# Ten input-projection pairs that copy their first and fifth product from bank to bank, nine of them with ten of sixteen k-tiles by sevens

## The chip, the cores and the metric

The kernel runs on one core of one Trainium2 chip. The metric is device microseconds of one execution, the median of several runs; lower is better. The engines are TensorE (PE for matmuls, PEld for its weight loads), VectorE (DVE), ScalarE (ACT), GpSimd (POOL) and SyncE (SP, which issues most of the loads). PSUM has eight banks of 128 x 512 float32; a matmul writes into one bank.

## What is computed

One layer of a decoder trunk on 256 rows of 2048 channels: a norm, one large input projection, three attention mixers side by side, gates, an output projection, then a gated feed-forward. The change lies in the input projection and in what takes its results:

```
h = rmsnorm(x, g_mix)
proj = h @ w_in                      # 256 x 2048 times 2048 x 12288
q, k, v = qkv[0], qkv[1], qkv[2]     # 16 heads of 128 each, in four groups of four
gates = sigmoid(proj[..., 3 * MIX_WIDTH:])   # three branches of 2048
...
merged = gates[0]*(o_a @ w_branch_a) + gates[1]*(o_b @ w_branch_b) + gates[2]*(o_c @ w_branch_c)
x = x + merged @ w_out
```

## The kernel before

**Products.** Rows are two tiles of 128 (t = 0, 1), the 2048 input channels are sixteen k-tiles of 128, output columns go in blocks of 512. Every operand is split into a high and a low part (`split`, L107: the cast to the high part on ScalarE, the difference as the low part on VectorE), and one product (`product`, L169) is three matmuls: high by high, high by low, low by high. A weight block of two k-tiles (128 x 1024) is split in one go by `parts` (L311); its parts lie in the tiles w_hi and w_lo, of which there are five each, and a tile is free again when its last product is done.

**Pairs.** Two blocks of 512 columns, A and B, are projected together by `project_pair` (L351). For eight of the sixteen k-tiles (chunks 0 and 1, `WC`) it uses seven products in place of eight for each two-by-two block of (row tile, k half) by (k half, column block): sums of weights are formed on VectorE, or by DMAs that add (tiles u, g_raw), and sums of the activations lie ready in `hs` (class `Both`, L294). In the code `form(bank, f, ...)` is product number f = 1 to 7, four products at a time (two chunks, two k-tiles); `rest` is a plain product of a weight block, four products (two k-tiles, two row tiles). The order is 1, 2, 5, two rests of column B, 6, a rest, 7, a rest, 3, two rests of column A, 4, two rests. That makes seven times four and eight times four, 60 products in a pair.

**Banks.** A pair has four banks: X and Y, in which column A ends, and Z and V, in which column B is put together. Before `acc2` is opened all four come from the pool `acc`, which has two banks named ps and two named qs: the Z and V of a pair are the two banks that were X and Y of the pair before (`in_turn`, L874). Product 1 is needed in X and in the end in Y, product 5 in Z and V. In the pairs of w_in, X and Z are copied to SBUF by ScalarE (`snapshot`, L326: s1 and z5), and VectorE adds them back later: L407 and L408 for column B, and L423 for c11 = Y + s1, which is the first half of the result. In the pairs of w_gu and w_out (`by_banks`, L348) ScalarE copies from bank to bank instead, Y from X (L376) and V from Z (L378), and the sums are finished in PSUM.

**Units.** The projection runs two blocks of 512 columns alone (v of head group 0, one gate), then eleven pairs: q and k of group 0 (called qk0 here), qk1, v of groups 1 and 2 (vv), qk2, qk3, v of group 3 with a gate (vg), and five pairs of gates (g1 to g5). Before g4 the attention's banks are closed and `acc2` gives Z and V banks of their own. `begin_pair` (L338) does the start of the next pair (loads, the splits of the first block, sums u, splits of the second) at the end of the one before.

**What runs beside.** Attention is cut into steps, which `parts` sets off one by one (`stages`, `slow_stages`). `keep_qk` (L845) takes the q and k results, `rows_to_columns` (L758) scales, normalizes and transposes them, `keep_v` (L828) takes v. The tile v has one buffer: v of group 1 is written (L838) when the last matmul of group 0's attention (L708, L709) has read the old one. `keep_gate_rows` (L810) applies the sigmoid and sends a gate out to memory. `split_o` (L881) splits the attention's output during g4 and g5.

**What sets the order.** The framework orders each engine's instructions at build time, by the program's order and by what would be ready in its own model of the times; some are pinned to the program's order (`keep_in_program_order`), all loads by SP among them (`fetch`, L103). On the chip each engine runs its list strictly in order and waits on semaphores.

Of the kernel before, what the change touches and what calls it, by code (L numbers as in the profile page):

```python
# [55 lines left out]
def hybrid_block(ctx: ExitStack, tc: tile.TileContext, x, w_in, w_branch, w_out, w_gu, w_down, rel_bias,  # L56
# [237 lines left out]
    class Both(Sums):  # L294


        def __init__(self, pl, cols, wc):
            super().__init__(pl, "b", wc, False)
            self.shared(pl)
            self.plain = cols.plain  # L300


    WC = (0, 1)

    def load(w, k, col0, pl=None):

        raw = pl.tile([P, 2, NB], F32, name="g_raw", bufs=6 if pl is gx else 4) if pl else wpool.tile([P, 2, NB], F32, name="w_raw", bufs=4)
        (nc.sync.dma_start if w is w_down else fetch)(raw, block(w, k, col0))
        return raw
# [27 lines left out]

    def begin_pair(acts, w, colA, colB):  # L338

        b11, b12 = (quarter(acts, w, 0, col0) for col0 in (colA, colB))  # L340
        p11 = [parts(b) for b in b11]
        u = [gx.tile([P, 2, NB], F32, name="u") for _ in acts.wc]
        for a, b, d in zip(b11, b12, u):
            nc.vector.tensor_add(d, a, b)  # L344
        b21 = quarter(acts, w, 1, colA)
        return p11, b12, u, b21, [parts(b) for b in (u if by_banks(w) else b21)]

    def by_banks(w):  # L348
        return w is w_gu or w is w_out

    def project_pair(acts, w, colA, colB, begun=None, nxt=None, by_dma=False, early=None):  # L351
# [7 lines left out]
        def form(ps, f, srcs, start, stop, split=False):  # L359
            for i, c in enumerate(acts.wc):  # L360
                wh, wl = srcs[i] if split else parts(srcs[i])
                for j in range(2):
                    product(ps, *acts.form(f, c, j), wh[:, j], wl[:, j], start and i + j == 0,
                            stop and i + j == len(acts.wc))
# [8 lines left out]
        p11, b12, u, b21, second = begun or begin_pair(acts, w, colA, colB)  # L373
        form(X, 1, p11, True, True, True)
        if by_banks(w):
            tc.keep_in_program_order(nc.scalar.copy(Y, X))  # L376
            form(Z, 5, second, True, True, True)
            doubled[:] = [tc.keep_in_program_order(nc.scalar.copy(V, Z))]  # L378
            form(Y, 2, b21, False, False)
        else:  # L380
            s1 = snapshot(X)
            form(Y, 2, second, True, False, True)
            form(Z, 5, u, True, True)
# [6 lines left out]
        rest(1, ks[0], Z, V, start=not by_banks(w), raw=plain[0])  # L390
# [6 lines left out]
        rest(1, ks[2], Z, V)  # L397
        if not by_dma:
            add_into(b12, b22)
        form(X, 7, b12, False, True)  # L400
        x3 = snapshot(X)
        rest(1, ks[3], Z, V, stop=True)
        c22 = half_kb()
        if by_banks(w):
# [4 lines left out]
        form(Z, 3, b22, False, True)  # L409
# [6 lines left out]
        form(X, 4, u, False, False)  # L416
# [3 lines left out]
        if by_banks(w):  # L420
# [59 lines left out]
    for c in range(2, 4):  # L480
        whole[c] = gx.tile([P, NT, 4, P], F32, name="g_raw", bufs=6)
# [104 lines left out]
    def load_rows():  # L586
        for t in range(NT):
            for n in range(2):
                rows.append(gx.tile([P, 2 * NB], F32, name="g_raw", bufs=6))
# [168 lines left out]
    def rows_to_columns(g, sbs, dst):  # L758
        for i in (0, 2, 3):
# [85 lines left out]
    def keep_qk(g, q0, q1, k0, k1):  # L845
        sbs = [q0, half_kb(), k0, k1]
        nc.scalar.activation(sbs[1], q1, AF.Copy, scale=rstd[:, 1:2])
# [16 lines left out]
    def pair_of(kind, what):  # L864
# [6 lines left out]
        if kind == "vg":  # L871
            return hs, w_in, V0 + what[0] * NB, gate_col(*what[1])

# [15 lines left out]
    for (kind, what), after in zip(units, units[1:] + [(None, None)]):  # L889
# [47 lines left out]
    pgx.close()  # L937
    tc.keep_in_program_order(nc.scalar.preload_act_table_set("natural_log_exp_and_others"))
# [372 lines left out]
```

## Time and profile before

| | |
|---|---|
| median of 3 runs | 1338.33 us (1338.18 to 1339.57) |
| the profiled execution | 1337.34 us |
| its span, first to last instruction | 1335.6 us |
| matmul instructions | 6243 |
| loads of w_in by SP | 103 + 88 of 512 KB |
| adding DMAs by POOL, into u, and into g_raw at L389 | 50 and 20 of 512 KB |

The profile is of one execution. Its views: the page (busy time of each engine, forty slices, the chain of work that ended last), groups of instructions by line, the timeline of an engine in a window, and a table of windows: for each stretch of time its length, then the busy time of each engine with the number of instructions in brackets, the granted TensorE clock, the share of the DMA engines and their GB/s. Busy times of neighbouring instructions overlap a little, so a price is read from start to start where instructions follow each other without a gap.

### The profile page before, as it was taken

Reading aid. Unit: us, or ns where it says so; the run is one execution under the profiler, and the core shown is the slowest. Engines: PE = TensorE matmul, PEld = TensorE weight load, DVE = VectorE, ACT = ScalarE, POOL = GpSimd, SP = SyncE. Lnnn points to the kernel's source line nnn. Section 1 sums busy time; section 2 is a strip of 40 time slices with the busy share of each in tenths; the row PEclk is TensorE's granted clock in tenths of the full one; section 3 lists DMA queues with packets and bytes.
Section 4 is the critical chain, followed back from the end, with each engine's and each line's share of the span. In section 5 each row is a group of like instructions: output and inputs, shape, how many; then the busy total and the mean of one; then the engine's idle time right before and its main releaser. Section 6 shows DMA issues by size and latency. Waiting matters only on the chain.

```text
span 1335.6 us, 17783 instructions
## 1 busy us (share of the span) xinstructions
PE 1328.6 (99%) x6243; PEld 1158.7 (87%) x6243; DVE 1168.9 (88%) x1254; ACT 940.9 (70%) x1209; POOL 130.9 (10%) x195
## 2 busy tenths in 40 slices
PE   9999999999999999999999999999999999999998
PEld 6888888888888888888888888888888888888887
DVE  7978898989888897986999999989899997998887
ACT  7786867788777776544777778777877875665563
POOL 1100110001111111100210000001000001001010
PEclk9999999999999999999999999999999999999999
DMA  9997878797788878877988889889899977789883
GB/s 359 308 282 246 263 210 258 252 277 223 263 267 282 277 241 289 294 249 244 305 312 267 259 265 278 238 252 308 279 286 274 281 216 253 252 276 301 270 271 96
DMA packets 119505, 354.70 MB, mean 266 GB/s; under 512 B 32832, under 2 KB 34552, under 8 KB 119416
## 3 DMA queue, kind: packets, MB, share of 16 engines
q1 hardware_dynamic: 77016, 277.45, 58.4%
q0 software_dynamic: 19984, 69.76, 22.2%
q10 hardware_dynamic: 22416, 6.36, 2.8%
q8 instruction: 49, 0.80, 0.2%
q14 instruction: 40, 0.33, 0.1%
HBM read 294.26 MB, written 14.70 MB: 231 GB/s over the span
## 4 chain that ended last, share of the span: by engine, by line
PE 98%; DMA 1%; ACT 0%; DVE 0%; SPq 0%; issue 0%; DVEq 0%
PE qs L172 12%; PE ps L173 12%; PE qs L174 12%; PE qs L173 12%; PE ps L174 12%; PE ps L172 12%; PE z L173 4%; PE z L172 4%; PE z L174 4%; PE v L172 2%; PE v L173 2%; PE v L174 2%; PE tr L174 1%; PE tr L172 1%; PE tr L173 1%; PE tr L205 1%
## 5 line engine op out<-in xcount | busy, mean ns | idle before, releaser
L108 DVE TENSOR_TENSOR w_lo<-w_raw,w_hi 128x1024 fp32r<-128x1024 f32 x302 | 366.0, 1220 | 57.9 <-ACT w_hi L108 56.6
L108 ACT CAST w_hi<-w_raw 128x1024 fp32r<-128x1024 f32 x302 | 313.7, 1047 | 111.3 <-PE qs L174 39.5
L108 ACT CAST w_hi<-g_raw 128x1024 fp32r<-128x1024 f32 x216 | 222.8, 1050 | 106.0 <-PE qs L174 32.9
L108 DVE TENSOR_TENSOR w_lo<-g_raw,w_hi 128x1024 fp32r<-128x1024 f32 x216 | 257.5, 1220 | 19.7 <-ACT w_hi L108 17.4
L108 ACT CAST w_hi<-u 128x1024 fp32r<-128x1024 f32 x162 | 168.7, 1049 | 107.1 <-PE qs L174 22.4
L108 DVE TENSOR_TENSOR w_lo<-u,w_hi 128x1024 fp32r<-128x1024 f32 x162 | 195.6, 1221 | 42.5 <-ACT w_hi L108 37.6
L173 PE MATMUL ps<-w_lo,h_hi 128*128 128x512 f32 x352 | 134.0, 381 | 0.5 <-DVE w_lo L108 0.5
L174 PE MATMUL ps<-w_hi,h_lo 128*128 128x512 f32 x352 | 133.5, 380 | 0.1
L172 PE MATMUL ps<-w_hi,h_hi 128*128 128x512 f32 x352 | 129.1, 382 | 0.0
L173 PE MATMUL qs<-w_lo,h_hi 128*128 128x512 f32 x332 | 126.5, 381 | 0.0
L174 PE MATMUL qs<-w_hi,h_lo 128*128 128x512 f32 x332 | 126.0, 380 | 0.0
L172 PE MATMUL qs<-w_hi,h_hi 128*128 128x512 f32 x332 | 121.3, 382 | 0.0
L173 PEld LDWEIGHTS ps<-w_lo,h_hi 128*128 128x128 f32 x352 | 66.5, 189 | 10.4 <-DVE w_lo L108 1.3
L174 PEld LDWEIGHTS ps<-w_hi,h_lo 128*128 128x128 f32 x352 | 66.5, 189 | 10.3 <-DVE h_lo L108 1.1
L395 POOL DMA_DIRECT2D u<-g_raw x46 | 40.1, 871 | 360.1 <-DVE w_lo L108 299.6
L172 PEld LDWEIGHTS ps<-w_hi,h_hi 128*128 128x128 f32 x352 | 66.3, 189 | 9.5 <-ACT h_hi L108 0.3
L172 PEld LDWEIGHTS qs<-w_hi,h_hi 128*128 128x128 f32 x332 | 62.7, 189 | 9.1 <-ACT sc L328 0.4
L173 PEld LDWEIGHTS qs<-w_lo,h_hi 128*128 128x128 f32 x332 | 62.8, 189 | 8.7
L174 PEld LDWEIGHTS qs<-w_hi,h_lo 128*128 128x128 f32 x332 | 62.8, 189 | 8.7
L344 DVE TENSOR_TENSOR u<-g_raw 128x1024 f32<-128x1024 f32 x46 | 56.0, 1219 | 13.1 <-DMA g_raw<-in_w_gu 9.5
L333 DVE TENSOR_TENSOR u<-u,g_raw 128x1024 f32<-128x1024 f32 x46 | 54.2, 1218 | 0.0
L389 POOL DMA_DIRECT2D g_raw<-g_raw x20 | 17.3, 867 | 252.2 <-DMA g_raw<-in_w_in 133.7
(440 smaller groups left out, 2977.2 us busy)
## 6 DMA issues: line engine op xcount, KB each, us to landing
w_raw<-in_w_in SPq DMA_DIRECT2D x103, 512.0 KB, 7.0
g_raw<-in_w_in SPq DMA_DIRECT2D x88, 512.0 KB, 6.2
g_raw<-in_w_gu SPq DMA_DIRECT2D x88, 512.0 KB, 6.2
w_raw<-in_w_gu SPq DMA_DIRECT2D x88, 512.0 KB, 6.4
w_raw<-in_w_down SPq DMA_DIRECT2D x56, 512.0 KB, 4.8
u<-g_raw POOLq DMA_DIRECT2D x50, 512.0 KB, 6.6
w_raw<-in_w_branch SPq DMA_DIRECT2D x32, 512.0 KB, 4.6
g_raw<-in_w_down SPq DMA_DIRECT2D x32, 512.0 KB, 5.0
```

What stands on the lines that cost most here:

```text
L108: cast, rest = nc.scalar.copy(hi, src), nc.vector.tensor_sub(lo, src, hi.bitcast(F32))
L172: nc.tensor.matmul(ps, ah, wh, start=start, stop=False, **how)
L173: nc.tensor.matmul(ps, ah, wl, start=False, stop=False, **how)
L174: nc.tensor.matmul(ps, al, wh, start=False, stop=stop, **how)
L205: nc.tensor.transpose(pt[:, i, :], src[:, i * P:(i + 1) * P], ident)
L333: tc.keep_in_program_order(nc.vector.tensor_add(d, d, a))
L344: nc.vector.tensor_add(d, a, b)
L389: nc.gpsimd.dma_start(d, a, accum_op=ALU.add)
L395: nc.gpsimd.dma_start(d, a, accum_op=ALU.add)
```

## The change

Ten of the eleven pairs of w_in (all but g4) now go by banks, as those of w_gu and w_out: `by_banks` takes the column. So s1, z5 and the adds L407 and L423 go, and c11 is no tile in SBUF any more but the bank Y: `keep_qk`, `keep_v` and `keep_gate_rows` read both halves of column A from PSUM on ScalarE. The order in such a pair is 1, 5, 2 at the start.

Nine of the pairs (`halved`: all but qk0 and qk2) take two more k-tiles, 8 and 9, by sevens: one product more in each of the seven forms, and two rests fewer. The sums of the activations for it are made once, by `put_half`, and stored where `hs` reads nothing (`spare`). The weights of k-tiles 8 and 9 are loaded by `begin_half` for both columns; the first (a) and the last (b, after an add) are split whole, the sum hu is split three times at half the width (`parts_of_half`). `keep_qk` scales both q halves at once, and `rows_to_columns` has one step less. The tile g_raw has 8 buffers in place of 6 during the projection.

```diff
+        def put_half(self, k, t0, t1):
+            self.half = k
+            a11, a12, a21, a22 = (a[:, kh:kh + 1, :] for a in (t0, t1) for kh in range(2))
+            nc.vector.tensor_sub(a22, a21, a22)
+            nc.vector.tensor_sub(a21, a11, a21)
+            nc.vector.tensor_sub(a11, a22, a11)
+            nc.vector.tensor_add(a12, a12, a11)
+            for t, a in enumerate((t0, t1)):
+                split(*self.spare(t), a)
...
+    def parts_of_half(src):
+        hi, lo = (wpool.tile([P, 2, NB], F32R, name=f"w_{n}")[:, 0] for n in ("hi", "lo"))
+        split(hi, lo, src)
+        return hi, lo
+
+    def begin_half(acts, w, colA, colB):
+        a, b = (load(w, acts.half, col0, gx) for col0 in (colA, colB))
+        pa_ = parts(a)
+        u = half_kb()
+        nc.vector.tensor_add(u, a[:, 0], b[:, 0])
+        return a, b, pa_, u
...
         p11 = [parts(b) for b in b11]
+        half = begin_half(acts, w, colA, colB) if w is w_in and colA in halved else None
...
-        return p11, b12, u, b21, [parts(b) for b in (u if by_banks(w) else b21)]
-
-    def by_banks(w):
-        return w is w_gu or w is w_out
+        return half, p11, b12, u, b21, [parts(b) for b in (u if by_banks(w, colA) else b21)]
+
+    def by_banks(w, colA):
+        return w is not w_in or colA != gate_col(*chunks[8])
...
+            if more:
+                product(ps, *acts.form_half(f), *more, False, stop)
...
-        form(X, 1, p11, True, True, True)
-        if by_banks(w):
+        if half:
+            ha, hb, hp, hu = half
+            ks.remove(acts.half)
+        form(X, 1, p11, True, True, True, half and half_of(hp, 0))
+        if by_banks(w, colA):
             tc.keep_in_program_order(nc.scalar.copy(Y, X))
-            form(Z, 5, second, True, True, True)
+            form(Z, 5, second, True, True, True, half and parts_of_half(hu))
             doubled[:] = [tc.keep_in_program_order(nc.scalar.copy(V, Z))]
-            form(Y, 2, b21, False, False)
+            form(Y, 2, b21, False, False, more=half and half_of(hp, 1))
...
+            if half:
+                nc.gpsimd.dma_start(hb[:, 0], hb[:, 1], accum_op=ALU.add)
...
-        form(X, 6, u, False, True)
+        if half:
+            nc.vector.tensor_add(hu, hu, hb[:, 1])
+        form(X, 6, u, False, True, more=half and parts_of_half(hu))
...
+        if half:
+            nc.gpsimd.dma_start(hu, ha[:, 1], accum_op=ALU.add)
...
+            if half:
+                nc.vector.tensor_add(hb[:, 0], hb[:, 0], hb[:, 1])
+        hq = parts(hb) if half else None
+        form(X, 7, b12, False, True, more=half and half_of(hq, 0))
...
+        form(Z, 3, b22, False, True, more=half and half_of(hq, 1))
...
+        form(X, 4, u, False, False, more=half and parts_of_half(hu))
...
     def rows_to_columns(g, sbs, dst):
-        for i in (0, 2, 3):
+        for i in (2, 3):
...
-        sbs = [q0, half_kb(), k0, k1]
-        nc.scalar.activation(sbs[1], q1, AF.Copy, scale=rstd[:, 1:2])
+        sbs = [half_kb(), half_kb(), k0, k1]
+        for t, q in ((1, q1), (0, q0)):
+            nc.scalar.activation(sbs[t], q, AF.Copy, scale=rstd[:, t:t + 1])
...
+    halved = {g * NB for g in (1, 3)} | {V0 + NB, V0 + 3 * NB} | {gate_col(*chunks[i]) for i in range(2, len(chunks), 2)}
...
+            if kind == "gate":
+                hs.put_half(8, *(a[:, 0:2] for a in columns[2]))
...
-            keep_gate_rows(c0, b0, 1, ps[1])
-            late = gates_late([(c0, b0, 0, ps[0]), (c1, b1, 0, ps[2]), (c1, b1, 1, ps[3])])
+            for t in (1, 0):
+                keep_gate_rows(c0, b0, t, ps[t])
+            late = gates_late([(c1, b1, t, ps[2 + t]) for t in range(NT)])
```

In the branches that aren't shown: the add of hb's halves goes by DMA where the other adds of the pair do (`by_dma`: qk0 to g3) and by VectorE in g4 and g5; g4 keeps the old order with the same extra product in each form; the rests' loops run over the three blocks that are left.

More of the change, by code (lines that the diff above doesn't have):

```diff
@@ L299, in __init__, with spare, form_half @@
             self.shared(pl)
-            self.plain = cols.plain
+            self.plain, self.cols, self.half = cols.plain, cols, None
+        def spare(self, t):
+            return [x[:, t:8:4, P:S] for x in (self.cols.hi, self.cols.lo)]
+        def put_half(self, k, t0, t1):
[7 more added lines that the diff above has]
+                split(*self.spare(t), a)
+        def form_half(self, f):
+            if f in SUM_AT:
+                kh, t = SUM_AT[f]
+                return [x[:, 4 * kh + t, P:S] for x in (self.cols.hi, self.cols.lo)]
+            return self.plain(*{1: (0, self.half), 2: (0, self.half + 1), 4: (1, self.half + 1)}[f])
     WC = (0, 1)
+    raw_bufs = [8]
     def load(w, k, col0, pl=None):
-        raw = pl.tile([P, 2, NB], F32, name="g_raw", bufs=6 if pl is gx else 4) if pl else wpool.tile([P, 2, NB], F32, name="w_raw", bufs=4)
+        raw = pl.tile([P, 2, NB], F32, name="g_raw", bufs=raw_bufs[0] if pl is gx else 4) if pl else wpool.tile([P, 2, NB], F32, name="w_raw", bufs=4)
         (nc.sync.dma_start if w is w_down else fetch)(raw, block(w, k, col0))
@@ L357, in project_pair, with form @@
         Z, V = others()
-        def form(ps, f, srcs, start, stop, split=False):
+        def form(ps, f, srcs, start, stop, split=False, more=None):
             for i, c in enumerate(acts.wc):
@@ L363, in form, with half_of @@
                     product(ps, *acts.form(f, c, j), wh[:, j], wl[:, j], start and i + j == 0,
-                            stop and i + j == len(acts.wc))
+                            stop and not more and i + j == len(acts.wc))
+            if more:
+                product(ps, *acts.form_half(f), *more, False, stop)
+        def half_of(p, j):
+            return [x[:, j] for x in p]
         def rest(n, k, p0, p1, start=False, stop=False, raw=None):
@@ L415, in project_pair @@
             rest(0, k, Y, X)
-        form(X, 4, u, False, False)
+        form(X, 4, u, False, False, more=half and parts_of_half(hu))
         for k in ks[2:]:
@@ L419, in project_pair @@
         ahead = begin_pair(*nxt) if nxt else None
-        if by_banks(w):
+        if by_banks(w, colA):
             return (Y, X, c12, c22), ahead
@@ L480, in hybrid_block @@
     for c in range(2, 4):
-        whole[c] = gx.tile([P, NT, 4, P], F32, name="g_raw", bufs=6)
+        whole[c] = gx.tile([P, NT, 4, P], F32, name="g_raw", bufs=raw_bufs[0])
     columns = {c: [whole[c][:, t] for t in range(NT)] for c in range(4)}
@@ L588, in load_rows @@
             for n in range(2):
-                rows.append(gx.tile([P, 2 * NB], F32, name="g_raw", bufs=6))
+                rows.append(gx.tile([P, 2 * NB], F32, name="g_raw", bufs=raw_bufs[0]))
                 fetch(rows[-1], x[t * P:(t + 1) * P, 2 * n * NB:2 * (n + 1) * NB])
@@ L937, in hybrid_block @@
     pgx.close()
+    raw_bufs[0] = 6
     tc.keep_in_program_order(nc.scalar.preload_act_table_set("natural_log_exp_and_others"))
```

17 lines of the change are left out of this document (8 added, 9 removed).

## The prediction

> **What bounds the kernel now.** I read the page first: the shares of the engines, the granted clock, the chain that ended last.
>
> ```profile
> span 1335.6 us, 17783 instructions
> PE 1328.6 (99%) x6243; PEld 1158.7 (87%) x6243; DVE 1168.9 (88%) x1254; ACT 940.9 (70%) x1209; POOL 130.9 (10%) x195
> PEclk9999999999999999999999999999999999999999
> PE 98%; DMA 1%; ACT 0%; DVE 0%; SPq 0%; issue 0%; DVEq 0%
> ```
>
> TensorE works for all but 7.0 us of the span, at full clock, and 98% of the last chain is its own work. What takes matmuls away saves time, as long as nobody else falls behind. VectorE with 88% is the next candidate, so I asked for the windows of the eleven pairs of w_in (qk0, qk1, vv, qk2, qk3, vg, g1 to g5, cut where each pair's last sum is formed), and of three later stretches for comparison.
>
> ```profile
> core 0: us, PE busy (x) PEld busy (x) DVE busy (x) ACT busy (x) POOL busy (x), PEclk, DMA share, GB/s
> 51.00:90.50 39.50, 39.50 (x184) 34.59 (x183) 33.73 (x36) 30.31 (x34) 4.64 (x6) 1.00 0.91 284
> 90.50:134.20 43.70, 43.70 (x214) 38.08 (x213) 36.94 (x38) 32.03 (x39) 4.08 (x5) 1.00 0.81 249
> 134.20:177.70 43.50, 43.50 (x207) 37.91 (x206) 37.16 (x45) 35.87 (x72) 2.80 (x4) 1.00 0.77 234
> 177.70:223.60 45.90, 45.90 (x230) 40.10 (x229) 39.52 (x49) 30.07 (x42) 5.05 (x6) 1.00 0.84 255
> 223.60:263.80 40.20, 40.20 (x192) 35.29 (x192) 36.10 (x47) 33.30 (x74) 3.33 (x4) 1.00 0.81 246
> 263.80:307.00 43.20, 43.20 (x217) 38.02 (x216) 39.74 (x58) 34.99 (x76) 4.14 (x5) 1.00 0.82 249
> 307.00:354.20 47.20, 47.20 (x237) 41.31 (x236) 42.62 (x55) 35.99 (x55) 6.18 (x8) 1.00 0.79 249
> 354.20:397.00 42.80, 42.80 (x209) 37.57 (x208) 35.84 (x41) 32.84 (x46) 5.67 (x8) 1.00 0.87 275
> 397.00:437.10 40.10, 40.10 (x189) 35.19 (x188) 32.95 (x30) 28.69 (x32) 4.84 (x7) 1.00 0.90 284
> 437.10:476.50 39.40, 39.40 (x184) 34.16 (x183) 37.02 (x35) 28.57 (x33) 3.99 (x6) 1.00 0.79 265
> 476.50:515.00 38.50, 38.50 (x180) 33.72 (x179) 33.91 (x32) 28.34 (x32) 5.12 (x8) 1.00 0.76 237
> 648.00:687.00 39.00, 38.86 (x189) 33.84 (x187) 37.99 (x44) 29.72 (x43) 5.30 (x9) 1.00 0.97 324
> 804.00:843.00 39.00, 39.00 (x182) 34.15 (x181) 36.48 (x36) 30.70 (x35) 1.74 (x2) 1.00 0.83 251
> 1120.00:1200.00 80.00, 80.00 (x372) 70.06 (x371) 77.43 (x81) 51.61 (x56) 5.23 (x9) 1.00 0.78 262
> ```
>
> In all eleven pairs TensorE is busy for the whole window; VectorE for 82% (g3) to 94% (g4). The slack that the change spends is VectorE's.
>
> **The matmuls removed.** k-tiles 8 and 9 cost eight products in a pair (two k-tiles, two row tiles, two columns), and seven afterwards; a product is three matmuls. Nine pairs: 27 matmuls. Their price is the distance of starts in a gapless stretch.
>
> ```profile
> 92.46 0.38 PE L174 MATMUL qs<-w_hi,h_lo 128*128 128x512 f32 x1
> ...
> 95.05 0.38 PE L174 MATMUL qs<-w_hi,h_lo 128*128 128x512 f32 x1
> ```
>
> Between these lie twelve steps, 2.59 / 12 = 0.216 us each. 27 x 0.216 = **5.8 us** less TensorE work; a halved pair is shorter by 0.65 us.
>
> **What VectorE gets.** The prices again from start to start.
>
> ```profile
> 291.52 0.69 DVE L407 TENSOR_TENSOR sc<-sc 128x512 f32<-128x512 f32 x1
> 292.12 1.22 DVE L108 TENSOR_TENSOR w_lo<-w_raw,w_hi 128x1024 fp32r<-128x1024 f32 x1
> ...
> 299.10 1.21 DVE L108 TENSOR_TENSOR w_lo<-w_raw,w_hi 128x1024 fp32r<-128x1024 f32 x1
> 300.23 1.21 DVE L344 TENSOR_TENSOR u<-g_raw 128x1024 f32<-128x1024 f32 x1
> ```
>
> A half-width operation takes 0.60 us, a whole one 1.13. The two splits of a and b replace those of two rests, so they cost nothing new. New in a halved pair are three half splits and two half sums for hu: 5 x 0.60 = 3.0 us; in g4 and g5, where hb's add isn't a DMA, six, 3.6 us. By banks, two half-width adds go (L407, L423): 1.2 us less in ten pairs. In sum (7 x 5 + 2 x 6 - 20) x 0.60 = 16.2 us more for VectorE, which by itself costs nothing while TensorE hides it. put_half (four sums of 128 columns, two differences of 256) comes once, before qk0, a pair that is relieved by 1.2 us; I take nothing for it, about 1.5 us at most.
>
> By pair, VectorE's busy time against the shortened window: qk1 38.7 of 43.0, vv 39.0 of 42.8, qk3 37.9 of 39.6, vg 41.5 of 42.6 (98%), g1 44.4 of 46.6 (95%), g2 and g3 under 90%, **g4 37.0 + 3.6 = 40.6 of 38.8**, g5 36.3 of 37.8 (96%). How full may VectorE be before TensorE waits? The last window above says 97% over 80 us without a gap, that at 648 us 97% with 0.14 us lost. So g4 alone is overdrawn, by 1.8 us; what VectorE has done ahead (the five w_lo tiles and the sums of begin_pair) covers part. At best it covers all of it, 0; at worst, at 97%, g4 needs 40.6 / 0.97 = 41.9, 3.1 us too many. I take 1.1, for g4 and g5 with vg together, nearer to the covered end, because g3 before it has 4.7 us spare to fill the tiles. Against that stands one thing: hp and later hq keep one of the five w_hi and w_lo tiles through three (two) forms, so the reserve is four tiles there.
>
> **ScalarE and the DMAs.** The groups by line show what a half-width copy costs on ScalarE, to SBUF and from bank to bank.
>
> ```profile
> L328 ACT COPY sc<-qs 128x512 f32<-128x512 f32 x36 | 21.0, 583 | 7.5 <-PE qs L174 7.3
> L376 ACT COPY qs<-qs x6: 572/602/603, 647.4 to 1038.5; 128x512 f32<-128x512 f32 x6
> ```
>
> ScalarE gets three half casts a pair, by these rows 0.6 us each, 1.8 us on at most 36 of 43.5: hidden. The copies from bank to bank stand in the place of the snapshots, at the same price, and run while TensorE does the next form (five products, 3.2 us). What is queued behind them on ScalarE are the casts of the next forms, already five tiles ahead. The loads are as many as before; two of them are issued earlier on SP's queue, ahead of the second block's, into the two added g_raw buffers. POOL gets two more adding DMAs of 256 KB in a by_dma pair. g3 (four adding DMAs of 512 KB) has a DMA share of 0.90 of 40.1 us, g4 (two) 0.79 of 39.4: 5.0 us for two, so the new ones take about 2.5 us and g3 reaches 0.98. qk0 runs at 0.91 and the window at 648 us at 0.97 with TensorE busy, so I take nothing; an overfull queue would cost at most that 2.5 us in g3.
>
> **What is late next: the banks.** By banks, product 5 comes second and needs the former X or Y, which now waits for ScalarE. The rows show such a copy after q and k (pair end 263.8) and after a gate (354.2):
>
> ```profile
> 264.75 0.69 ACT L847 ACTIVATE sc<-ps,rstd 128x512 f32<-128x512 f32 x1
> ...
> 355.32 1.28 ACT L812 ACT_TABLE_LOAD   x1
> 356.62 0.69 ACT L812 ACTIVATE sc<-ps,rstd 128x512 f32<-128x512 f32 x1
> ```
>
> After q and k X is free 1.6 us after the pair's end: harmless, since the first form takes 2.6 us, or 3.2 in a halved pair. After the gate it is free at 357.3, 3.1 us after the end: nothing, or some tenths. Whatever stands behind product 5 in TensorE's list waits with it. After vv it matters:
>
> ```profile
> 177.74 0.68 DVE L423 TENSOR_TENSOR sc<-ps,sc 128x512 f32<-128x512 f32 x1
> 180.88 2.49 DVE L779 TENSOR_TENSOR sc<-sc,rr 128x512 f32<-128x512 f32 x4
> 182.12 0.38 PE L172 MATMUL ps<-w_hi,hi 128*128 128x512 f32 x1
> 184.72 1.04 PE L205 MATMUL tr<-ident,sc 128*128 128x128 f32 x8
> 189.16 0.70 PE L708 MATMUL tr<-p,v 128*128 128x256 f32 x2
> 191.26 0.72 ACT L838 ACTIVATE v<-sc,rstd 128x512 f32<-128x512 f32 x1
> 191.88 0.68 ACT L838 ACTIVATE v<-ps,rstd 128x512 f32<-128x512 f32 x1
> ```
>
> Today L423 frees bank Y when vv ends, and product 5 of qk2 starts in it at 182.12. X waits until 191.88: v has one buffer, group 0's attention reads it in L708, and L708 stands behind the transposes (L205) of what L779 scales. With the change Y waits too. vv ends 1.3 us earlier, at about 175.9; without Z and V TensorE has products 1 and 2 (5.2 us), perhaps 6 (2.6), the transposes and L708 (about 3): 184 to 187. If L708 stays where it is, the first copy ends at 192.0 and TensorE loses up to 7.8 us, less 2.6 if product 6 fits in. If transposes and L708 follow L779 at once (8 transposes 1 us, VectorE's reads of them 1.2, L708 1.2, a copy 0.7), Z is free at about 186 and nothing is lost. I take 1.2: the order is laid out anew, so TensorE's own list puts ready work into the hole, and `rows_to_columns` is one step shorter.
>
> On such a hole the Trainium skill has a rule, "TensorE: Matmul & The Clock Gate", section "What's actually happening": after an idle window of about 3.4 us the array runs at half its clock until it has been busy for as long. By an estimate from that page a whole hole would cost some 1.7 us on top; with holes of 1.2 us nothing. No row here shows it: the clock is 1.00 in every window above.
>
> **The sum.** -5.8 + 1.1 + 1.2 = -3.5 us. The profiled execution took 1337.34, so 1333.8 on its terms; it lay 0.99 under the median of the runs, 1338.33. Forecast: **1334.8 us**, with 1333.0 to 1335.6 as this case's own range.
>
> **The rivals.** (1) No stall at all: 1338.33 - 5.8 = 1332.5. For it speak the windows at 97%, against it g4's overdraft. (2) The hole after vv in full, as a wait in the place of the one that L423 ended: -5.8 + 7.8 + 1.1 = +3.1, less some filling: 1338 to 1341, no measurable change. For it: one buffer for v, L708's late place. Against it: the new order. The DMA queue of g3 (2.5 us) alone would bring the forecast to 1337.3, into the same class. (3) The other side: VectorE becomes the bound. If it can't be busier over a pair than in the regular pairs of w_gu (36.48 of 39.0, 93.5%), because each of its splits waits for a cast first, then the pairs need qk3 40.5 (+0.9), vg 44.4 (+1.8), g1 47.5 (+0.9), g4 43.4 (+4.6), g5 38.8 (+1.0): 9.2 us, and the time is 1341.7. It decides from a limit below some 94%; the 77.43 of 80 at 1120 us speak against it, the shorter reserve of split tiles for it.
>
> **The chances.** A measurement can tell about 0.2%, 2.7 us. Forecast 0.43, rival 1 0.15: faster 0.58. Rival 2 and its like 0.27: same. Rival 3, or holes that add up beyond 8.5 us, 0.15: slower. The range leaves out about 0.15 above and a little below: 1332.4 (nothing lost) to 1340.8 (rival 2 nearly whole).
>
> **What the new profile would show.** 6216 matmul instructions. From bank to bank 22 copies of the kind of L376, no L407 or L423 outside g4. VectorE near 100% in g4 and TensorE's busy time short of the window there by about 1 us; a hole in front of product 5 of qk2 at 182 to 187 us, with a wait for ScalarE's copy to v. It would be wrong if that hole is 4 us or more, if holes lie in vg, g1 and g5 too, or if the DMA share is 1.00 in g3 with waits for loads behind it.

## The result, and the profile after

The changed kernel takes 1358.33 us (median of 4 runs, 1356.17 to 1360.12) where the kernel before takes 1338.37 beside it: 1.0147 times as long, with a 95% interval of 1.0135 to 1.0159. The profile of after is of the run that took 1360.12. Forecast were 1334.8 us and a range that ended at 1340.8. The change removes 5.8 us of matmuls and costs 20.0, so **25.8 us of TensorE's time are lost** where the forecast had 2.3.

The head of the page after, its slices of the granted clock, and the shares of the chain that ended last:

```profile
span 1358.4 us, 17797 instructions
PE 1335.3 (98%) x6216; PEld 1155.9 (85%) x6216; DVE 1185.8 (87%) x1287; ACT 957.9 (71%) x1238; POOL 144.5 (11%) x211
PEclk9999989999999999999999999999999999999999
PE 82%; DVE 8%; ACT 3%; DMA 3%; issue 2%; SPq 0%; DVEq 0%; ACTq 0%
```

The matmuls are 6216, as the 27 fewer should give. But the chain, 98% of it TensorE's before, now runs through VectorE, ScalarE and DMAs for 14%. VectorE worked 16.9 us more (1185.8 against 1168.9), and its share of the longer span is not higher.

Both kernels cut at the same marks, the starts of the instruction that forms c12 (L411 before, L463 after, first step of column B's result). A window holds the end of one pair and most of the next: qk1, vv, qk2, qk3, vg, g1 to g5, and the stretch to the first branch. First the kernel before, of which four windows and the sum will do:

```profile
core 0: us, PE busy (x) PEld busy (x) DVE busy (x) ACT busy (x) POOL busy (x), PEclk, DMA share, GB/s
...
123.02:166.97 43.95, 43.95 (x209) 37.99 (x208) 37.61 (x42) 34.97 (x71) 3.42 (x4) 1.00 0.74 221
166.97:209.93 42.96, 42.96 (x211) 37.37 (x211) 40.12 (x56) 29.43 (x40) 4.18 (x5) 1.00 0.82 246
...
427.04:464.54 37.50, 37.50 (x174) 32.52 (x173) 33.78 (x33) 27.04 (x31) 3.99 (x6) 1.00 0.78 254
464.54:504.02 39.48, 39.48 (x184) 34.58 (x183) 37.00 (x36) 28.67 (x33) 5.12 (x8) 1.00 0.77 251
...
sum 437.50, PE 437.50 PEld 382.73 DVE 383.65 ACT 329.53 POOL 45.49; mean PE 39.77 PEld 34.79 DVE 34.88 ACT 29.96 POOL 4.14
```

Then the changed kernel, without four windows in which TensorE is idle for 1.4 us together:

```profile
core 0: us, PE busy (x) PEld busy (x) DVE busy (x) ACT busy (x) POOL busy (x), PEclk, DMA share, GB/s
...
122.78:170.57 47.79, 45.44 (x203) 38.01 (x202) 39.73 (x46) 37.00 (x74) 5.16 (x6) 0.96 0.75 218
170.57:221.51 50.94, 46.41 (x216) 39.92 (x215) 41.03 (x52) 32.64 (x45) 4.17 (x5) 0.93 0.69 222
...
265.95:311.28 45.33, 44.54 (x218) 38.31 (x217) 41.63 (x62) 36.11 (x79) 5.85 (x7) 1.00 0.90 273
311.28:356.43 45.15, 44.92 (x228) 39.30 (x227) 43.97 (x61) 37.86 (x59) 7.10 (x9) 1.00 0.90 277
...
401.50:439.96 38.46, 38.46 (x178) 33.34 (x177) 34.82 (x33) 29.57 (x35) 7.43 (x10) 1.00 0.93 290
439.96:482.16 42.20, 39.41 (x181) 33.71 (x180) 37.58 (x38) 29.11 (x35) 4.84 (x7) 1.00 0.81 267
482.16:524.92 42.76, 39.60 (x176) 32.31 (x175) 39.69 (x41) 29.68 (x35) 4.83 (x7) 1.00 0.69 215
...
sum 457.89, PE 442.66 PEld 379.27 DVE 401.21 ACT 346.46 POOL 58.07; mean PE 40.24 PEld 34.48 DVE 36.47 ACT 31.50 POOL 5.28
```

The stretch is 20.4 us longer, of 22.8 between the two spans, so nearly all that counts happens in these pairs. Four windows hold most of it: vv 3.8 us longer, qk2 8.0, g4 4.7, g5 3.3. TensorE is idle for 15.2 us (457.89 - 442.66); before, for none. Its busy time should be 431.7 after the cut (437.50 - 5.8) and is 11 us more: the clock accounts for half of that (0.04 of 47.79 us and 0.07 of 50.94 are 5.5 us), the rest is spread over matmul records that I couldn't split further. And a reading on which much turns: **over the windows in which TensorE waits, VectorE is not full.** It is busy for 83% of the vv window, 81% of qk2's, 89% of g4's, 93% of g5's. The waits themselves lower these shares. Against the windows of the kernel before, less 0.65 us where the pair is halved, VectorE's work is 92% in vv, 96% in qk2 and 102% in g4 and g5 together (the marks fall a little differently in the two kernels). So at the end of the row VectorE has more to do than TensorE; in vv and qk2 it hasn't, and yet they lose most.

The hole after vv in the timeline of after (start, duration, engine, line; in brackets the idle time before and what ended it):

```profile
184.98 2.49 DVE L831 TENSOR_TENSOR sc<-sc,rr 128x512 f32<-128x512 f32 x4
187.17 1.04 PE L205 MATMUL tr<-ident,sc 128*128 128x128 f32 x8
187.39 2.35 DVE L108 TENSOR_TENSOR w_lo<-w_raw,w_hi 128x1024 fp32r<-128x1024 f32 x2
189.66 2.35 DVE L354 TENSOR_TENSOR u<-u,g_raw 128x1024 f32<-128x1024 f32 x2
190.98 1.04 ACT L108 CAST w_hi<-u 128x1024 fp32r<-128x1024 f32 x1 [3.86 <-DVE u L354]
192.08 0.79 PE L172 MATMUL qs<-w_hi,hi 128*128 128x512 f32 x1 [3.87 <-ACT w_hi L108]
193.57 1.06 PE L760 MATMUL tr<-p,v 128*128 128x256 f32 x2
196.86 1.27 ACT L890 ACTIVATE v<-ps,rstd 128x512 f32<-128x512 f32 x2
198.46 0.46 PE L172 MATMUL ps<-w_hi,hi 128*128 128x512 f32 x1
```

TensorE is out of work for 3.87 us: the next product (the sixth, for product 5 has no bank yet) needs a cast, the cast needs a sum u, and VectorE makes that sum only after L831 and two splits that stand ahead of it. VectorE waits for nothing here; from 182.62 to 194.3 us it works without a gap. L760, which must read v before the new v may leave its bank, comes at 193.57, L890 empties the banks at 196.86, and product 5 gets its bank at 198.46. Now short windows of the same place:

```profile
186.00:190.00 4.00, 2.21 (x15) 1.76 (x13) 4.00 (x6) 1.05 (x1) 0.00 (x0) 1.00 0.08 6
190.00:194.00 4.00, 1.92 (x6) 1.53 (x7) 4.00 (x5) 1.23 (x2) 0.00 (x0) 0.64 0.67 256
194.00:198.00 4.00, 4.00 (x13) 3.37 (x12) 0.34 (x1) 2.03 (x4) 0.86 (x1) 0.51 0.55 110
```

VectorE is full in the hole itself, for 4.00 of 4.00 us twice: it is a burst, not the average, that TensorE meets. The granted clock falls to 0.64 and 0.51 behind the idle time, so what TensorE then has runs at about half speed. In vv it falls too, behind two shorter idle times (0.54 us before 154.18 and 1.52 before 156.18):

```profile
154.00:158.00 4.00, 2.30 (x7) 1.75 (x8) 4.00 (x5) 4.00 (x16) 1.30 (x2) 0.87 0.46 146
158.00:162.00 4.00, 4.00 (x14) 3.27 (x14) 3.48 (x5) 3.42 (x5) 0.41 (x1) 0.70 1.05 207
```

The other kind of wait, in the window of g4 of after:

```profile
440.57 1.22 DVE L108 TENSOR_TENSOR w_lo<-u,w_hi 128x1024 fp32r<-128x1024 f32 x1
445.94 0.69 DVE L368 TENSOR_TENSOR sc<-g_raw 128x512 f32<-128x512 f32 x1 [4.16 <-DMA g_raw<-in_w_in]
446.55 1.22 DVE L108 TENSOR_TENSOR w_lo<-u,w_hi 128x1024 fp32r<-128x1024 f32 x1
447.82 0.48 PE L173 MATMUL ps<-w_lo,h_hi 128*128 128x512 f32 x1 [1.43 <-DVE w_lo L108]
```

L368 is the first sum for hu, made for the *next* pair. It stands in VectorE's list ahead of a split that the *current* pair needs, and waits there 4.16 us for a load; TensorE is short by 1.43 at once. The source view of that line, and the waits of SP's queue from 30 to 530 us (total, times, longest), first after, then before:

```profile
L368 DVE TENSOR_TENSOR sc<-g_raw x9: 681/693/694, 84.6 to 485.8; 128x512 f32<-128x512 f32 x9
...
  DMA g_raw<-in_w_in: 10.7, 6
```

```profile
SPq L105 <- DMA sc<-g_raw: 53.0, 8, 8.9
SPq L105 <- DMA u<-g_raw: 38.7, 16, 6.9
```

```profile
SPq L105 <- DMA u<-g_raw: 8.6, 8, 1.7
```

Six of the nine sums wait, 10.7 us in all. SP's queue, which is in order, now stands for 53.0 us before tiles that the new adding DMAs into hu (from ha, L443) have yet to read, and 30 us longer than before at those into u. That this makes the loads late is argued, not shown: a longer stand at one place can be a shorter one at another (before VectorE's splits, L108, the queue stands 274.6 us in place of 325.6).

### The profile page after: what moved, and what is told of

Same layout as the page of the kernel before. It is cut to its first block, busy times and chain, and to the rows that moved or that the text cites. A ratio compares the mean times of both kernels' runs of the same rounds, so it can differ in the third digit from the quotient of the medians.

```text
span 1358.4 us, 17797 instructions
## 1 busy us (share of the span) xinstructions
PE 1335.3 (98%) x6216; PEld 1155.9 (85%) x6216; DVE 1185.8 (87%) x1287; ACT 957.9 (71%) x1238; POOL 144.5 (11%) x211
## 4 chain that ended last, share of the span: by engine, by line
PE 82%; DVE 8%; ACT 3%; DMA 3%; issue 2%; SPq 0%; DVEq 0%; ACTq 0%
PE ps L173 10%; PE ps L174 10%; PE ps L172 10%; PE qs L172 10%; PE qs L173 10%; PE qs L174 10%; DVE w_lo L108 5%; PE z L173 3%; PE z L172 3%; PE z L174 3%; PE v L172 2%; PE v L174 2%; PE v L173 2%; ACT w_hi L108 2%; DMA g_raw<-in_w_in 2%
## 5 line engine op out<-in xcount | busy, mean ns | idle before, releaser
L108 DVE TENSOR_TENSOR w_lo<-w_raw,w_hi 128x1024 fp32r<-128x1024 f32 x284 | 343.9, 1220 | 53.1 <-ACT w_hi L108 51.4
L108 ACT CAST w_hi<-w_raw 128x1024 fp32r<-128x1024 f32 x284 | 295.0, 1047 | 107.5 <-PE qs L174 35.6
L108 ACT CAST w_hi<-g_raw 128x1024 fp32r<-128x1024 f32 x234 | 241.3, 1049 | 98.9 <-DVE g_raw L354 29.6
L108 DVE TENSOR_TENSOR w_lo<-g_raw,w_hi 128x1024 fp32r<-128x1024 f32 x234 | 279.2, 1221 | 22.2 <-ACT w_hi L108 20.2
L108 ACT CAST w_hi<-u 128x1024 fp32r<-128x1024 f32 x162 | 168.4, 1049 | 118.8 <-DVE u L354 25.7
L108 DVE TENSOR_TENSOR w_lo<-u,w_hi 128x1024 fp32r<-128x1024 f32 x162 | 195.5, 1221 | 34.1 <-ACT w_hi L108 31.9
L354 DVE TENSOR_TENSOR u<-u,g_raw 128x1024 f32<-128x1024 f32 x46 | 54.2, 1218 | 0.0
L172 PE MATMUL qs<-w_hi,hi 128*128 128x512 f32 x108 | 41.9, 388 | 3.9 <-ACT w_hi L108 3.9
```

Source lines behind the costliest of these rows:

```text
L108: cast, rest = nc.scalar.copy(hi, src), nc.vector.tensor_sub(lo, src, hi.bitcast(F32))
L172: nc.tensor.matmul(ps, ah, wh, start=start, stop=False, **how)
L354: tc.keep_in_program_order(nc.vector.tensor_add(d, d, a))
```

## The experiments

My theories at first were the banks (the hole after vv) and the late loads, with the amount of VectorE's work as their rival; from e10 on the reserve of split tiles came in. "Over before" is the median less that of the kernel before on the same chip (1337.76 to 1338.55).

| run | what is changed | median us | ratio to before, 95% | over before |
|---|---|---|---|---|
| after | | 1358.33 | 1.0147 [1.0135, 1.0159] | +20.0 |
| e1 | after, bank copies only | 1340.22 | 1.0016 [1.0007, 1.0026] | +2.1 |
| e2 | after, extra k-tiles only | 1352.13 | 1.0105 [1.0090, 1.0120] | +14.0 |
| e3 | after, vv in the old order | 1355.75 | 1.0141 [1.0124, 1.0158] | +17.6 |
| e4 | after, hu's second add by VectorE | 1363.17 | 1.0186 [1.0171, 1.0202] | +25.0 |
| e5 | after, hu's first sum later | 1352.00 | 1.0104 [1.0089, 1.0119] | +13.8 |
| e6 | after, hu without a low part | 1351.04 | 1.0101 [1.0086, 1.0116] | +12.8 |
| e7 | before, 45 free adds | 1344.81 | 1.0049 [1.0034, 1.0064] | +6.6 |
| e8 | after, hu's low parts by POOL | 1360.87 | 1.0163 [1.0146, 1.0180] | +22.6 |
| e9 | before, 45 adds that read u | 1347.07 | 1.0061 [1.0047, 1.0075] | +8.5 |
| e10 | before, four w_hi and w_lo tiles | 1343.88 | 1.0039 [1.0025, 1.0052] | +5.3 |
| e11 | e5 and e3 | 1349.31 | 1.0078 [1.0063, 1.0094] | +10.8 |
| e12 | vg, g1, g2, g3 only, late sum | 1336.04 | 0.9978 [0.9968, 0.9988] | -2.5 |
| e13 | neither part, after's text | 1337.35 | 0.9995 [0.9986, 1.0005] | -0.8 |
| e14 | e13 with vv halved | 1336.64 | 0.9989 [0.9980, 0.9998] | -1.5 |
| e15 | e14 without a low part | 1336.94 | 0.9994 [0.9984, 1.0003] | -1.2 |
| e16 | e13 with g4, g5 | 1339.03 | 1.0010 [1.0000, 1.0019] | +0.9 |
| e17 | e13 with qk1 and vv halved | 1342.13 | 1.0031 [1.0020, 1.0042] | +4.4 |
| e18 | e12 and vv in the old order | 1335.25 | 0.9979 [0.9970, 0.9988] | -2.5 |

### The two halves of the change (e1, e2)

e1 empties `halved`; e2 takes the copies from bank to bank away again.

```diff
-    halved = {g * NB for g in (1, 3)} | ...
+    halved = set()
```

```diff
     def by_banks(w, colA):
-        return w is not w_in or colA != gate_col(*chunks[8])
+        return w is not w_in
```

> No pair is halved (eight k-tiles by sevens everywhere, as before); ten pairs still copy from bank to bank. Theory banks (after vv, product 5 of qk2 waits until ScalarE has copied Y and X to the one buffer of v): the hole after vv stays, some 8 us, the other holes go: 1344 to 1348 us. Theory loads (k-tiles 8 and 9 come late, because the queue of loads waits for a buffer that an adding DMA still reads, and VectorE waits in order for them): the same here, 1344 to 1348. Rival VectorE (it has too much work in the pairs): it is relieved by 12 us against the kernel before, so 1338 or less.

> Nine pairs are halved, but no pair of w_in copies from bank to bank: products 1, 2, 5 in that order, s1 and z5 in SBUF. Theory banks: the hole after vv goes, about 8 us less than the changed kernel, 1348 to 1352. Theory loads: the holes at vv's start and in g4 and g5 stay, so still well above 1338. Rival VectorE: it gets 11 us more work than in the changed kernel, so 1360 or more.

e1 is 2.1 us over before and e2 14.0, together 16.1 of the 20.0. The extra k-tiles cost most of it, 14.0 + 5.8 = 19.8 us of holes; the two parts seem to make each other worse by 3.9, about twice what one such ratio is uncertain by. That e1 costs anything is telling: VectorE's busy time falls by 8.5 us (1160.4 against 1168.9; twenty adds go, and the six operations of `put_half` come), and no matmul goes. VectorE's work alone can't be the measure. e1 also shows the bank's own part of the hole after vv: there TensorE waits 0.66 us at 181.91 for the copy into Y and 0.24 at 186.75, in place of 3.87 for a sum.

### The hole after vv (e3) and the adding DMA (e4)

```diff
-        return w is not w_in or colA != gate_col(*chunks[8])
+        return w is not w_in or colA not in (gate_col(*chunks[8]), V0 + NB)
```

```diff
-            nc.gpsimd.dma_start(hu, ha[:, 1], accum_op=ALU.add)
+            nc.vector.tensor_add(hu, hu, ha[:, 1])
```

> The changed kernel, but the pair vv alone goes the old way (s1 and z5 in SBUF, c11 formed by VectorE, which frees bank Y at once). Theory banks: the interval from vv's to qk2's column-B sum, 50.9 us in the changed kernel and 43.0 before, comes back to 43 to 45, and the time falls by 6 to 8 us to 1350 to 1352. If the hole after vv has another cause: 1358 within 2 us.

> The changed kernel, but hu + ha (half width, nine times) is added by VectorE and not by a DMA, so that ha's buffer is free some 8 us earlier. Theory loads: the waits of SP's queue for that adding DMA (53 us in eight waits) go, the loads of the next pair come earlier, and the holes in g4 and g5 and at vv's start shrink: 1349 to 1355. Rival VectorE: nine times 0.6 us more for it, 1359 to 1364.

With the old order in vv, Y is free early as before, and only 2.4 us come back, which isn't clear of the noise (1.0124 to 1.0158 beside 1.0135 to 1.0159). The hole was not just the bank's: in e3 TensorE still waits 3.02 us at 191.07 for the cast of a sum u, which is late without the bank too. e4 doesn't free ha's tile early, as it was meant to: SP's queue waits 34.9 us for VectorE's add and 55.5 for the DMAs into u, and L368 waits 12.6 us. So it doesn't settle whether the queue matters. It does give a price: nine half adds on VectorE, 9 x 0.60 = 5.4 us of work, cost 5.0 us more.

### The waits for loads (e5)

```diff
     def begin_half(acts, w, colA, colB):
...
-        u = half_kb()
-        nc.vector.tensor_add(u, a[:, 0], b[:, 0])
-        return a, b, pa_, u
+        return a, b, parts(a), half_kb()
...
             ks.remove(acts.half)
+            tc.keep_in_program_order(nc.vector.tensor_add(hu, ha[:, 0], hb[:, 0]))
```

> The changed kernel, with the sum hu = a + b moved from the end of the pair before to the place just ahead of its first split, and pinned there, so that VectorE no longer waits in it for loads while work of the old pair stands behind it (10.7 us in six waits). Theory loads: 1348 to 1353. Theory VectorE work (in the halved pairs VectorE's amount of work sets the pace): the work is the same, 1355 to 1360.

The same instructions with one sum per pair in a later place: 6.2 us less. The sum waits for no load there, while SP's queue stands about as long as in after (51.2 us before the DMAs into hu, 36.4 before those into u). That part of the loss is shown to be order, neither work nor the queue's waits by themselves.

### How much VectorE's work is worth (e6, e7, e8, e9, e10)

e6 leaves the 27 half-width differences away, e8 gives them to POOL:

```diff
     def parts_of_half(src):
...
-        split(hi, lo, src)
-        return hi, lo
+        nc.scalar.copy(hi, src)
+        return hi, hi
```

```diff
-        split(hi, lo, src)
+        nc.scalar.copy(hi, src)
+        nc.gpsimd.tensor_sub(lo, src, hi.bitcast(F32))
```

> The changed kernel; the three half splits of a pair make no low part (the high part is used twice), so 27 half-width operations, 16.2 us, are taken from VectorE; matmuls, loads and DMAs are the same. Part left out: the low part of hu. Theory VectorE work: the time falls by most of that, to 1343 to 1348. Theory loads: 1353 to 1358.

> The changed kernel; the low parts of the 27 half splits are computed by GpSimd in place of VectorE, all else alike. Theory VectorE work: VectorE is relieved by 16.2 us, and if GpSimd is in time the time falls as in e6_half_no_low, to 1343 to 1350; if GpSimd is late behind its queue of adding DMAs, it is no better than the changed kernel. Theory loads: 1353 to 1360.

e6 leaves 16.2 us of VectorE's work out (27 x 0.60), and 7.2 us come back: less than half, so there is something besides work, and the 12.8 that stay aren't explained by it. Nor need all of the 7.2 be work, for these splits take no w_lo tile either. POOL is no help, as its group in e8 shows (busy total and mean ns, then the idle time before them):

```profile
L362 POOL TENSOR_TENSOR w_lo<-sc,w_hi 128x512 fp32r<-128x512 f32 x27 | 49.4, 1831 | 132.1 <-ACT w_hi L361 132.0
```

At 1.83 us apiece the low part takes over a microsecond longer than on VectorE, and the median is 2.6 us above after's, which isn't clear of the noise. Nor is VectorE relieved: with 27 instructions fewer it is busy for 1186.2 us (1185.8 in after), and some of its own operations take longer, the 46 sums u at L354 for instance 1335 ns in the mean in place of 1218.

The other way round, e7 and e9 add five half-width operations to VectorE in each of nine pairs of the kernel *before*:

```diff
+            nc.vector.tensor_sub(ballast, ballast, ballast)
```

```diff
+            nc.vector.tensor_sub(ballast, u[0][:, 0], u[0][:, 1])
```

> The kernel before, with five half-width VectorE operations without use put into each of the nine pairs that the change halves (45 x 0.60 = 27 us; nothing depends on them, no load or bank is touched). With the ten pairs by banks the change itself adds 16.2 us, without them 28 (e2_halves_only). Theory VectorE work: 8 to 14 us slower than before, as e2_halves_only. Theory loads or banks: within 2 us of before.

> As e7_before_ballast (the kernel before with 45 useless half-width operations on VectorE), but each now reads the sum u of its own pair, so that it runs where hu's work runs in the changed kernel and not at the start. 27 us of VectorE work, no load, bank, cast or tile of weights touched. Theory VectorE work: 8 to 14 us slower than before, in the nine pairs' intervals. If it is within 3 us, VectorE's amount of work isn't the cause by itself, and the reserve of split tiles or the loads are.

```profile
L342 DVE TENSOR_TENSOR ballast<-u x45: 679/684/694, 87.4 to 500.3; 128x512 f32<-128x512 f32 x45
```

e7 missed: its operations wait for nothing, so the order put all of them between 1.5 and 112.5 us, and the 6.6 us say nothing of the pairs. In e9 they lie from 87.4 to 500.3 us: 27 us of work cost 8.5. By the prediction's rule (VectorE up to 97% is free) they should have cost 2.8 us, nearly all at vg and g4: (39.74 + 3.0) / 0.97 - 43.20 is 0.9, and (37.02 + 3.0) / 0.97 - 39.40 is 1.9. e10 holds one of the five w_hi and one of the five w_lo tiles of the kernel before from the end of qk0 to the end of g5:

```diff
+            held = [wpool.tile([P, 2, NB], F32R, name=f"w_{n}") for n in ("hi", "lo")]
```

> The kernel before, in which one of the five w_hi and one of the five w_lo tiles is kept occupied from the end of qk0 to the end of g5. No work is added but six tiny operations. Theory reserve (in the changed kernel hp and hq keep one of five tiles for three and two forms, and each half split takes a whole tile, so a burst on VectorE or ScalarE reaches TensorE sooner): 6 to 15 us slower, spread over the pairs with attention work. Theory VectorE work alone, or loads: within 3 us of before.

With four tiles of each and not a product or a sum more (but for a few tiny instructions that hold them) the kernel before loses 5.3 us, a little less than the 6 to 15 expected. It has no more reserve than it needs. The change keeps a tile for hp and then hq through several forms of each halved pair; what that costs in the changed kernel no run shows by itself.

### Which pairs (e11 to e18)

From here on the first sum for hu stands where e5 has it. e11 joins e5 and e3. The other runs differ in these two definitions:

```diff
e12
+        return w is not w_in or colA in halved
+    halved = {V0 + 3 * NB} | {gate_col(*chunks[i]) for i in (2, 4, 6)}
e13
+        return w is not w_in
+    halved = set()
e14, and e15 with the edit of e6
+        return w is not w_in
+    halved = {V0 + NB}
e16
+        return w is not w_in or colA == gate_col(*chunks[10])
+    halved = {gate_col(*chunks[i]) for i in (8, 10)}
e17
+        return w is not w_in
+    halved = {NB, V0 + NB}
e18
+        return w is not w_in or colA in halved and colA != V0 + NB
+    halved = {V0 + NB, V0 + 3 * NB} | {gate_col(*chunks[i]) for i in (2, 4, 6)}
```

> The changed kernel with both mends: hu's sum late (e5_late_hu_sum, -6.3 us against the changed kernel) and vv in the old order (e3_vv_old_order, -2.6). If the two causes are separate: 1349.4 within 1.5 us. If the late sum relieves VectorE ahead of vv's end, the hole after vv goes with it: 1345 or less.

> Only vg, g1, g2 and g3 are halved and by banks, with the late sum; the other pairs of w_in are as before. 12 matmuls go, 2.6 us. By e5's intervals (vg -2.0, g1 +1.8, g2 -1.1, g3 -1.8 against before) 1335 to 1337; theory VectorE work: vg and g1 are full to 95 to 98%, so 1337 to 1340.

e11 is 9.2 us better than after, where e5 and e3 alone bring 6.2 + 2.4: they add up, as two separate losses would. e12 halves four pairs (12 matmuls, 2.6 us) and is faster than before. I then went from both ends, with e13 as the control.

> The changed kernel's text, with no pair halved and no pair of w_in by banks: left are keep_qk's scaling of both halves, rows_to_columns one step shorter, the order of the first gates and eight buffers for g_raw. If these cost something by themselves (ScalarE's squares now fall into the start of vv): 1340 to 1344, with vv and qk2 longer by 2 to 5 us. If not: 1338.4 within 1.5.

> e13_neither with vv halved, in the old order, with the late sum: three matmuls fewer, 3.0 us more for VectorE in a pair that it filled to 85% over its window but to 100% in its second half. Theory VectorE work in the pair: 3 to 8 us above e13_neither, in vv and qk2. Theory that the costs add up from pair to pair (the reserve comes into vv already used up by qk1): within 1.5 us of e13_neither.

> e14_vv_alone without the low part of the three half splits (left out: the low part of hu), 1.8 us less for VectorE in vv. Theory VectorE work: at least half of what e14_vv_alone loses comes back. Theory tile reserve: the tiles are taken as long as before, so the loss stays within 1 us of e14_vv_alone.

> e13_neither with only g4 and g5 halved (g5 by banks, g4 in the old order, as in the changed kernel), with the late sum. Six matmuls fewer, 1.3 us. The prediction's overdraft (g4 needs 40.6 us of VectorE in 38.8): 1 to 3 us of holes, so 1338 to 1340 beside e13_neither; if what comes before them was the cause, 1337 or e13_neither less 1.3.

> e13_neither with qk1 and vv halved, both in the old order, late sum. Six matmuls fewer, 1.3 us. Theory that the backlog of VectorE is handed from pair to pair (vv alone costs nothing): 4 to 9 us above e13_neither, in vv and qk2, so 1341 to 1346. If two halved pairs in a row cost no more than one: 1336 to 1337.5.

> e12_four_pairs with vv halved too, in the old order. 15 matmuls fewer, 3.2 us, and qk1 before vv as it was: 1335.0 to 1336.0 if vv gains as alone; 1338 or more if vv's backlog reaches vg and g1 over qk2 and qk3, which aren't halved.

vv halved alone (e14) is 0.7 us better than the control, as its three matmuls (0.65) should make it, though that is no more than the noise; in its profile TensorE is busy throughout the windows of vv and qk2. So vv, whose window is 3.8 us longer in the changed kernel, costs nothing by itself, and leaving the low part out (e15) gives nothing further. g4 and g5 (e16) are 1.7 over the control where 1.3 less were due: **3.0 us lost, about the prediction's worst case for g4 (3.1)**. But the hole is not in g4. The windows of g4 and g5 in e16, cut at its own marks:

```profile
426.87:465.02 38.15, 38.15 (x179) 33.38 (x178) 35.97 (x37) 27.55 (x33) 4.83 (x7) 1.00 0.84 278
465.02:505.67 40.65, 38.96 (x176) 32.69 (x175) 40.00 (x41) 29.60 (x35) 4.83 (x7) 1.00 0.71 221
```

All of TensorE's idle time in the pairs, 1.69 us, lies in g5, and there VectorE is busy for 98% of the window. By these rows fill is the limit here, as the prediction had it for g4. (The profiles of e16 and e13 place 1.9 of the 3.0 us in these pairs; the rest stays unexplained.) qk1 and vv together (e17) are 5.2 over the control, 6.5 with their six matmuls. The loss lies in vv, whose window takes 48.28 us in e17 and 43.32 in e13, while that of qk1 takes 45.66 and 45.67: what happens in the pair before decides. Two windows of ten microseconds within vv, in e14 and then in e17:

```profile
141.00:151.00 10.00, 10.00 (x50) 8.82 (x49) 7.86 (x9) 10.00 (x27) 0.55 (x1) 1.00 0.75 176
151.00:161.00 10.00, 10.00 (x48) 8.43 (x48) 9.91 (x13) 8.80 (x26) 2.05 (x3) 1.00 0.91 193
```

```profile
141.00:151.00 10.00, 10.00 (x47) 8.31 (x46) 5.99 (x7) 8.54 (x22) 0.86 (x1) 1.00 0.83 181
151.00:161.00 10.00, 7.67 (x34) 5.56 (x33) 9.70 (x13) 7.64 (x19) 1.71 (x2) 1.00 0.68 160
```

In e17 VectorE has four microseconds free in the first window and is then full, while TensorE waits. The timeline of e17 has the reason:

```profile
149.57 0.96 DVE L734 SCALAR_TENSOR_TENSOR pT<-att,p 128x768 f32<-128x768 f32 x1 [1.12 <-ACT p L732]
150.56 0.96 DVE L736 SCALAR_TENSOR_TENSOR p<-att,p 128x768 f32<-128x768 f32 x1
151.44 0.75 DVE L739 TENSOR_TENSOR pT<-pT,before 128x256 f32<-128x256 f32 x2
152.11 2.35 DVE L354 TENSOR_TENSOR u<-u,g_raw 128x1024 f32<-128x1024 f32 x2
153.36 1.04 ACT L108 CAST w_hi<-u 128x1024 fp32r<-128x1024 f32 x1 [3.82 <-DVE u L354]
156.51 0.48 PE L173 MATMUL ps<-w_lo,hi 128*128 128x512 f32 x1 [1.57 <-DVE w_lo L108]
```

A step of the attention (L734 to L739) waits 1.12 us for ScalarE and then works for 2.5, the sums u stand behind it in VectorE's list, a cast waits 3.82 us for them, and TensorE 1.57 for the split that follows. The changed kernel has the same lines and the same hole in vv, at 149.24 to 156.18. In all three places an instruction that TensorE needs soon stands behind others: in g4 behind one that waits for a load, after vv behind ones that work, here behind both. No run halves qk1 alone, so it isn't shown that it takes two neighbours. Nor do neighbours always cost: e12 halves vg to g3, four in a row, and TensorE is busy throughout their windows.

e18, e12 with vv halved in the old order, is again 2.5 us faster than before, and the two can't be told apart; both beat both kernels. In e18 VectorE is *fuller* than in the changed kernel (the windows of qk2 and g1, cut at its own marks, and the sum):

```profile
168.11:209.15 41.04, 41.04 (x204) 36.09 (x203) 39.28 (x53) 29.97 (x41) 4.17 (x5) 1.00 0.80 242
...
296.92:345.34 48.42, 48.42 (x253) 42.88 (x252) 46.46 (x68) 40.75 (x71) 7.11 (x9) 1.00 0.83 247
...
sum 434.12, PE 434.12 PEld 379.71 DVE 393.03 ACT 333.66 POOL 54.12; mean PE 39.47 PEld 34.52 DVE 35.73 ACT 30.33 POOL 4.92
```

VectorE is busy for 96% of both windows and for 393.03 of all 434.12 us (91%, against 88% in after, whose 401.21 us are more work in a longer time), and TensorE isn't idle at all: 434.12 us of work, 3.4 less than before for 15 fewer matmuls (3.2).

## Why the prediction was wrong

**Right.** The matmuls and their price: 6216, and in e14 and e18 the time that they should bring. The 22 copies from bank to bank, at 0.57 to 0.60 us. That VectorE is overdrawn at the end of the row, though in g5 and not in g4. That the banks leave a hole after vv, and about its size: by e1 0.9 us where 1.2 were taken. That the DMA engines themselves aren't the limit: g3's window has a share of 0.93 and TensorE busy throughout. Of the prediction's signs of being wrong, one came: holes lie in vg, g1 and g5 too.

**The step that failed first: "97% over 80 us without a gap ... so g4 alone is overdrawn".** I read from steady windows how full VectorE may be, and from that took 1.1 us for all pairs. That rule holds where it is reached: no wait at 96% in e18, 1.69 us at 98% in g5 of e16. But vv and qk2 stay below it (92 and 96% of the windows of before) and lose 11.8 us of the 20.4. A pair's average is not a sufficient test. The list is fixed and in order; what counts too is how much stands ahead of an instruction that TensorE needs soon, working or waiting, and how many split tiles lie ready meanwhile. e9 and e10 show how little room the kernel before has for both (8.5 us for 27 us of work, 5.3 us for a fifth of the tiles), e17 that what is put into qk1 is paid for in vv, which a sum by pairs can't hold.

**"The loads are as many as before; two of them are issued earlier" was costed at nothing.** I counted the DMAs, not who stands behind them. L368 waits for one in six of nine pairs, with the current pair's splits behind it; e5 measures 6.2 us. For the banks I asked what is queued behind a waiting instruction; for this sum I didn't.

**The hole after vv, "I take 1.2".** The window of qk2 is 8.0 us longer, which looks like the full hole of 7.8. But by e1 the banks alone make a hole of 0.9 us, and by e3 the bank of vv is worth about 2.4; the rest is VectorE's list again. What I relied on, that the order would put ready work into the hole, did not happen: there was no ready work, since the sum u was late. The clock then fell to 0.64 and 0.51 in two windows of 4 us, 1.4 and 2.0 us of full clock. The rule from the Trainium skill that the prediction weighed, "TensorE: Matmul & The Clock Gate", section "What's actually happening", is half the clock after an idle window of about 3.4 us; it agrees here, after 3.87 us idle, though the loss is twice the prediction's estimate of 1.7 by the Trainium skill. In vv it doesn't agree: the clock was 0.87 and 0.70 behind idle times of 0.54 and 1.52 us, another 1.7 us of full clock, where the prediction had nothing for short holes.

**g4 and g5, part of the 1.1**, should have had the upper end, 3.1: e16 has 3.0, but in g5, to which the prediction gave 36.3 of 37.8 us, 96%; in its profile VectorE is busy there for 98%. In after this doesn't show so plainly, for L368 waits 4.16 and 2.93 us in these two windows.

**The rival that VectorE becomes the bound** named the side and was too small (1341.7), since it too was a fill, of 93.5%.

**The account of the 25.8 us**, by differences over before with the matmuls added:

| | us | by |
|---|---|---|
| first sum for hu, and vv's bank order | 9.2 | after to e11 |
| g4 and g5 | 3.0 | e16 to e13 |
| qk1 ahead of vv | 6.5 | e17 to e13 |
| qk3, and the bank copies in qk0 to qk3 | 6.4 | what is left between e11 and e18 |
| five halved pairs, vv and vg to g3 | 0.7 | e18 to before |

From e11 to e18, holes go from 10.8 + 5.8 = 16.6 to -2.5 + 3.2 = 0.7, so 15.9; less 6.5 and 3.0 leaves 6.4. The rows between come from different surroundings and needn't add up so neatly. In e11's profile the place of what is left is the window of qk2, behind vv, rather than qk3's: 3.4 us of idle TensorE and 1.9 of lowered clock there, against 0.5 in qk3's. **What stays open:** how the 6.4 are divided, and, within the losses of e17 and qk2, how much is VectorE's extra work, how much the shorter reserve and how much the order. The runs show that each can matter, work in e4, e6 and e9, the order in e5, the reserve in e10 (in the kernel before alone), and none that was tried accounts for the whole.

## What to carry to other kernels

When TensorE is at 99% and a helper engine at 88%, don't only ask how full the helper may be, but walk through its list at every place that the change adds an instruction: what does it wait for, what stands behind it, and how long does TensorE live on the tiles that are ready. Put sums for the next pair behind the current pair's splits, and test a change in one pair and in two neighbours, because a pair can pay for the one before it (e17). Where a change of many places fails, some of the places may still be worth having: four or five of these pairs give 2.5 us.

## What the runs showed of the hardware

The clock's fall to about half after an idle time of 3.87 us, and that the lowered clock cost up to 5.5 us over the whole run, was more than I had reckoned with. It also fell in vv behind idle times of 0.54 and 1.52 us, while in e17 nearly the same (0.48 and 1.57) left it at 1.00. A difference of 128 x 512 float32 took POOL 1831 ns in the mean in e8, beside 683 ns on VectorE in after, 2.7 times as long, and VectorE's own sums at L354 went from 1218 to 1335 ns beside it. The Trainium skill, "GPSIMD Engine Reference", section "3.1 Elementwise — side-by-side cycle accounting", has 1.96 for an add of 2048 elements; here the measured ratio is the worse one, with VectorE busy for 87% of the time beside it. And SP's in-order load queue stood for up to 8.9 us at a time before a tile that an adding DMA had yet to read. The DMA itself took 3.2 to 6.1 us from issue to landing (the nine at L443); before it POOL waited 61.5 us in seven of them for VectorE's splits.
